# Another order of products, and a transfer in place of a sum, in the last group of a two-layer attention trunk

## The chip, the cores and the metric

The kernel runs on one core of one Trainium2 chip. The metric is the device time of one execution in microseconds (us); the time of a kernel is the median of its runs. TensorE does the matrix products, VectorE (DVE in the rows) and ScalarE (ACT) the elementwise work, GpSimd (POOL) issues some of the transfers and SyncE (SP) most of them.

## The reference

Two layers over 256 tokens of 2048 channels. Each layer normalises its input and multiplies it by one wide weight matrix; two causal token mixers work on the result, and their gated outputs are merged and added to the residual stream.

```python
h = rms_norm(x, norm_gain)
proj = jnp.einsum('bsd,de->bse', h, w_in)
(da_q, da_k, da_v, da_z, sb_q, sb_k, sb_v, sb_z,
 gate_a, gate_b) = split_columns(proj)
...
ub = stick_breaking_attention(qs, ks, vs) * jax.nn.silu(sb_z)

y = (jax.nn.sigmoid(gate_a) * jnp.einsum('bse,ed->bsd', ua, w_branch_a)
     + jax.nn.sigmoid(gate_b) * jnp.einsum('bse,ed->bsd', ub, w_branch_b))
return x + jnp.einsum('bsd,de->bse', y, w_out)
```

Everything is float32. The segments of `proj` that matter here are `sb_v` and `sb_z` (2048 columns each) and the two gates.

## The kernel before

**Precision.** A float32 product is made of three TensorE matmuls (`mm3`, lines 70 to 72): each operand is split into a high part, rounded by ScalarE (line 65, tiles `wh`), and a low part, subtracted by VectorE (line 66, tiles `wl`). A weight slice of 128 x 1024 (512 KB, two k-steps of 512 columns) is loaded by SyncE's queue (line 93) into one of 12 `raw` buffers, split, and used. There are 4 buffers `wh` and 3 `wl`.

**Two kinds of streams.** A `c_stream` multiplies the 256 tokens by one chunk of 512 columns in 8 steps of 12 matmuls (`mc` in the accumulator memory). An `s_stream` makes two chunks at once, with seven products of half depth in place of eight (Strassen's scheme in Winograd's form): 28 steps of 6 matmuls. Its weight halves are b11, b21 (first chunk) and b12, b22 (second chunk), four slices each. The left-hand sums s(0) to s(3) were made earlier (`sm`); the right-hand sums are made in place, in the raw buffers of b11 (`xs`) and b22 (`zs`), slice by slice, each after the step that has read the slice's old value. Such a sum is either an accumulating transfer, issued on GpSimd's queue (line 169, b12 or b22 is read again from memory and added), or one VectorE instruction on two buffers (line 173). The accumulators are sU, sN and sQ, one buffer each.

**The two orders.** A flag `tb_dma` chooses.

With the flag, the products follow as a(0,0) into sU; s(3) into sN, each step followed by the transfer zs += b12; s(0) into sQ, each step followed by the transfer xs += b22; s(2) into a new sQ; s(1) into sU, added to what is there; a(1,0) into sN; a(1,1) into sQ.

Without it, s(3) is followed by nothing; each step of s(0) is followed by the VectorE sum xs += zs and then by the transfer zs += b12; s(1) comes before s(2). In both cases ScalarE copies s(0)'s result out of sQ into p5 (line 218) before sQ is used again, and VectorE's lines 227, 230 and 236 take the results of s(1), s(3) and s(2) on.

**Where they run.** Each layer has four stick-breaking groups of four heads. For group g, `sb_weights(g)` makes the attention weights (scores; lines 659 to 670 on ScalarE and VectorE; transposes on TensorE at line 548), then one `s_stream` makes the group's `sb_v` and `sb_z` chunks, interleaved by `run` with a chain of two `c_stream`s of 8 steps and 2 idle steps each: the next group's queries and keys, whose results are transposed on TensorE (line 277), or, in the last group, two chunks of gate a, whose results go through a sigmoid (line 716) to memory (line 717). `run` advances the stream that is behind, 20 steps against 28. The last group also splits reloaded values `ua`. Behind the last group come three more `s_stream`s for gates, without the flag, interleaved with the branch products (the gate blocks).

The program is laid out by a planner that simulates it and orders each engine's instructions by priority; splits and sums are raised in priority. So an engine's order isn't always that of the text.

Of the kernel before, what the change touches and what calls it, by code (L numbers as in the profile page):

```python
# [23 lines left out]
NG = D // CW  # L24
# [18 lines left out]
def trunk(ctx: ExitStack, tc: tile.TileContext, x, xT, norm_gain, w_in, qk_gain, lam_vecs,  # L43
# [14 lines left out]
    def heads(ap):  # L58
        return ap.rearrange("p (h d) -> p h d", d=HD)
# [196 lines left out]
    def run(*streams):  # L256

        live = [[n, 0, g] for n, g in streams]
        while live:
            s = min(live, key=lambda s: (s[1] + 0.5) / s[0])  # L260
            if next(s[2], "end") == "end":
                live.remove(s)
            s[1] += 1

    def chain(*gens):
        for g in gens:
            yield from g
# [144 lines left out]
    for l in range(DEPTH):  # L412
# [37 lines left out]
        def w_chunk(base, g):  # L450
            return [w_in[l, base + g, kp] for kp in range(KP)]
# [133 lines left out]
        def vz_fin(v, gz, after_z=None):  # L585

            def fin_v(t, op):
                n = tok()
                op(n)
                split(v[0][:, t], v[1][:, t], n)  # L590

            def fin_z(t, op):
                op(gz[:, t])
                if t == NT - 1:
                    gf = gz.rearrange("p t d -> p (t d)")
                    nc.scalar.activation(out=gf, in_=gf, func=AF.Silu)
                    if after_z is not None:
                        after_z()
            return fin_v, fin_z
# [18 lines left out]
        def v_tiles():  # L618
            return (att.tile([P, NT, CW], F32R, name="vh"), att.tile([P, NT, CW], F32R, name="vl"))
# [32 lines left out]
        def sb_weights(g):  # L652
            wT = attn_pair()
            table(EXP_LN)
            for t in range(NT):
                for hs in ([[0, 1, 2, 3]] if t == 0 else [[0, 1], [2, 3]]):
                    sm, nk = scores(qT[NG + g], kT[NG + g], hs, t, masks["strict"])
                    e = tok()
                    nc.scalar.activation(out=e, in_=sm, func=AF.Abs)
                    nc.scalar.activation(out=e, in_=e, func=AF.Exp, scale=-1.0)  # L660
                    nc.scalar.activation(out=e, in_=e, func=AF.Ln, bias=1.0)
                    rl = tok()
                    nc.scalar.activation(out=rl, in_=sm, func=AF.Relu)
                    for i in range(len(hs)):
                        lo, hi = i * nk, (i + 1) * nk
                        rv = slice(hi - 1, lo - 1 if lo else None, -1)
                        nc.vector.tensor_tensor_scan(out=e[:, rv], data0=e[:, rv], data1=rl[:, rv],
                                                     initial=0.0, op0=ALU.add, op1=ALU.add)
                    nc.vector.tensor_tensor(out=sm, in0=sm, in1=e, op=ALU.subtract)
                    nc.scalar.activation(out=sm, in_=sm, func=AF.Exp)  # L670
                    attn_T(sm, wT, hs, t)
            return wT

        def sb_out(g, wT, v, gzT):
            keep = g == NG - 1
            if keep:
                uh, ul = u_parts()
            else:
                us = att.tile([P, HPG, S], F32, name="us", tag="aTh")
            for hp in range(0, HPG, 2):  # L680
                o = ps_at.tile([P, CW], F32, name="at")
                ov = o.rearrange("p (h q) -> p h q", q=S)
                for i in range(2):
                    h = hp + i
                    vs = slice(h * HD, (h + 1) * HD)
                    mm3(ov[:, i], v[0][:, 0, vs], v[1][:, 0, vs], wT[0][:, h, 0:2].rearrange(
                        "p b q -> p (b q)"), wT[1][:, h, 0:2].rearrange("p b q -> p (b q)"),
                        True, False)
                    mm3(ov[:, i, P:], v[0][:, 1, vs], v[1][:, 1, vs], wT[0][:, h, 2], wT[1][:, h, 2],
                        False, True)  # L690
                hs = slice(hp, hp + 2)
                uv = tok().rearrange("p (h q) -> p h q", q=S) if keep else us[:, hs]
                nc.vector.tensor_tensor(out=uv, in0=ov, in1=gzT[:, hs], op=ALU.mult)
                if keep:
                    split(uh[:, hs], ul[:, hs], uv)
            if keep:
                return uh, ul
            spill("b", g, us)
# [30 lines left out]
        def q_stream(n, xin, alt=False, gap=0):  # L729
            f, base = (da_fin, DA_Q) if n < NG else (sb_fin, SB_Q)  # L730
            return c_stream(w_chunk(base, n % NG), xin, f("q", n % NG), alt, gap)

        def k_stream(n, xin, alt=False, gap=0, before=None):
            f, base = (da_fin, DA_K) if n < NG else (sb_fin, SB_K)
            return c_stream(w_chunk(base, n % NG), xin, f("k", n % NG), alt, gap, before)
# [27 lines left out]
        def reload(b, groups, u):  # L763
            for g in groups:
                raw = load_raw(u_dram[b][:, g * 4:(g + 1) * 4].rearrange("p h s -> p (h s)"))
                ts = [att.tile([P, 4, S], F32R, name="u" + b, tag=tag) for tag in GZ_TAGS[g]]
                split(ts[0], ts[1], raw.rearrange("p (h s) -> p h s", s=S))
                for i in range(2):
                    u[i][g] = ts[i]

        def gate_chunk(b, c):
            return c_stream(w_chunk(GATE_A if b == "a" else GATE_B, c), xt, sig_fin(b, c), False,
                            GAP)

        ua, ub = ([None] * NG, [None] * NG), ([None] * NG, [None] * NG)
        for g in range(NG):
            wT = sb_weights(g)
            if g == NG - 1:
                reload("a", (0, 1), ua)
            v = v_tiles()  # L780
            gz = att.tile([P, NT, CW], F32, name="gz")
            gzT = []

            def z_T():
                gzT.append(att.tile([P, HPG, S], F32, name="gzT", tag="hold"))
                for t in range(NT):
                    tr = ps_at.tile([P, CW], F32, name="at")
                    for h in range(HPG):
                        nc.tensor.transpose(out=tr[:, h * P:(h + 1) * P],
                                            in_=gz[:, t, h * P:(h + 1) * P], identity=ident)  # L790
                    nc.scalar.copy(gzT[0][:, :, t * P:(t + 1) * P], heads(tr))

            fv, fz = vz_fin(v, gz, z_T)
            s = s_stream(w_chunk(SB_V, g), w_chunk(SB_Z, g), xt, sm,
                         lambda col, t, op: (fv, fz)[col](t, op), g + 1 < NG)
            if g + 1 < NG:
                c = [q_stream(NG + g + 1, xt, False, GAP), k_stream(NG + g + 1, xt, False, GAP)]
            else:
                c = [gate_chunk("a", 0), gate_chunk("a", 1)]
            run((len(c) * (C_STEPS + GAP), chain(*c)), (S_STEPS, s))  # L800
            last_u = sb_out(g, wT, v, gzT[0])
# [154 lines left out]
```

## Time and profile before

| | |
|---|---|
| median of 3 runs | 2382.98 us (2380.82 to 2383.87) |
| the profiled execution | 2380.12 us, span 2378.4 us |
| instructions | 31466 |
| TensorE matmul busy | 2356.9 us, 99% of the span |
| VectorE, ScalarE, GpSimd busy | 1781.6, 1529.9 and 341.1 us |
| read from memory, written | 509.35 and 24.12 MB |

The profiled execution is one of its own, not among the three runs. Its span runs from the first to the last recorded instruction. Busy shares are of the span; TensorE's matmuls overlap, so their starts tell more than their lengths.

### The profile page before, as it was taken

What the parts mean: (1) busy time and instruction counts of PE and PEld (TensorE: products, weight loads), DVE (VectorE), ACT (ScalarE), POOL (GpSimd) and SP (SyncE); (2) the same over time, 40 slices, a digit from 0 to 9 for tenths busy, and PEclk for the clock granted to TensorE, in tenths of its full rate; (3) what the DMA queues carried; (4) which work ended last, traced back from release to release, by engine and by line L of the source; (5) the groups of instructions that cost most, each with busy time, mean ns of one, the idle gap of its engine ahead of it and who ended that gap; (6) DMA issues with size and microseconds to landing.
All of it is one profiled execution on the core that took longest, in us unless ns stands there. A gap on an engine that the chain in (4) does not pass through costs nothing.

```text
span 2378.4 us, 31466 instructions
## 1 busy us (share of the span) xinstructions
PE 2356.9 (99%) x10996; PEld 1955.5 (82%) x10996; DVE 1781.6 (75%) x2000; ACT 1529.9 (64%) x2201; POOL 341.1 (14%) x399
## 2 busy tenths in 40 slices
PE   9999999999999999999999999999999999999999
PEld 7888888888888888788888888888888888887887
DVE  6777768688788888786566777676887887878854
ACT  7666666677777666554465666666767776656643
POOL 1231220201101011100020312202011010111000
PEclk9999999999999999999999999999999999999999
DMA  9546546878877888898665465468789778988972
GB/s 367 179 143 210 196 142 221 198 224 235 238 234 209 266 274 247 293 287 271 207 211 177 142 213 187 141 226 209 224 233 241 234 210 254 289 237 285 298 264 89
DMA packets 152239, 535.55 MB, mean 225 GB/s; under 512 B 17360, under 2 KB 17872, under 8 KB 152080
## 3 DMA queue, kind: packets, MB, share of 16 engines
q1 hardware_dynamic: 123552, 432.72, 53.3%
q0 software_dynamic: 28096, 100.42, 19.9%
q8 instruction: 86, 1.41, 0.2%
q14 instruction: 73, 0.60, 0.1%
q10 hardware_dynamic: 432, 0.40, 0.1%
HBM read 509.35 MB, written 24.12 MB: 224 GB/s over the span
## 4 chain that ended last, share of the span: by engine, by line
PE 96%; DMA 2%; DVE 1%; ACT 1%; issue 0%; DVEq 0%; SPq 0%; ACTq 0%
PE mc L71 16%; PE mc L72 16%; PE mc L70 16%; PE sU L71 6%; PE sU L72 5%; PE sU L70 5%; PE sN L71 5%; PE sN L72 5%; PE sN L70 5%; PE sQ L71 3%; PE sQ L70 3%; PE sQ L72 3%; PE at L277 2%; PE at L71 1%; PE at L72 1%; PE at L70 1%
## 5 line engine op out<-in xcount | busy, mean ns | idle before, releaser
L66 DVE TENSOR_TENSOR wl<-raw,wh 128x1024 fp32r<-128x1024 f32 (+1 forms) x1001 | 1212.5, 1222 | 391.9 <-PE mc L71 155.9
L65 ACT CAST wh<-raw 128x1024 fp32r<-128x1024 f32 (+1 forms) x1001 | 1047.5, 1051 | 642.2 <-PE mc L72 340.7
L169 POOL DMA_DIRECT2D raw<-in_w_in x136 | 117.8, 867 | 835.4 <-DVE wl L66 429.3
L71 PE MATMUL mc<-wl,xTh 128*128 128x512 f32 x576 | 225.1, 391 | 2.5 <-DVE wl L66 2.4
L72 PE MATMUL mc<-wh,xTl 128*128 128x512 f32 x576 | 224.4, 390 | 0.0
L70 PE MATMUL mc<-wh,xTh 128*128 128x512 f32 x576 | 206.8, 391 | 0.0
L70 PE MATMUL mc<-wh,xrh 128*128 128x512 f32 x512 | 197.6, 393 | 5.7 <-ACT wh L65 5.7
L71 PE MATMUL mc<-wl,xrh 128*128 128x512 f32 x512 | 200.5, 392 | 0.0
L72 PE MATMUL mc<-wh,xrl 128*128 128x512 f32 x512 | 200.3, 392 | 0.0
L71 PEld LDWEIGHTS mc<-wl,xTh 128*128 128x128 f32 x576 | 108.1, 188 | 26.2 <-DVE wl L66 4.2
L70 PEld LDWEIGHTS mc<-wh,xTh 128*128 128x128 f32 x576 | 107.7, 188 | 22.7 <-ACT wh L65 0.6
L72 PEld LDWEIGHTS mc<-wh,xTl 128*128 128x128 f32 x576 | 108.2, 188 | 21.9
L70 PEld LDWEIGHTS mc<-wh,xrh 128*128 128x128 f32 x512 | 96.6, 189 | 25.5 <-ACT wh L65 5.7
L173 DVE TENSOR_TENSOR raw<-raw 128x1024 f32<-128x1024 f32 x88 | 107.2, 1221 | 13.3 <-DMA raw<-in_w_in 12.2
L71 PEld LDWEIGHTS mc<-wl,xrh 128*128 128x128 f32 x512 | 96.6, 189 | 19.5 <-DVE wl L66 0.2
L72 PEld LDWEIGHTS mc<-wh,xrl 128*128 128x128 f32 x512 | 96.5, 188 | 19.3
L71 PE MATMUL sU<-wl,xrh 128*128 128x512 f32 x256 | 100.7, 393 | 0.1
L72 PE MATMUL sN<-wh,xrl 128*128 128x512 f32 x256 | 100.3, 392 | 0.0
L70 PE MATMUL sN<-wh,xrh 128*128 128x512 f32 x256 | 100.1, 391 | 0.0
L71 PE MATMUL mc<-wl,ua 128*128 128x512 f32 x256 | 100.0, 390 | 0.0
L71 PE MATMUL sN<-wl,xrh 128*128 128x512 f32 x256 | 100.0, 390 | 0.0
L70 PE MATMUL sU<-wh,xrh 128*128 128x512 f32 x256 | 100.0, 390 | 0.0
(254 smaller groups left out, 4913.6 us busy)
## 6 DMA issues: line engine op xcount, KB each, us to landing
raw<-in_w_in SPq DMA_DIRECT2D x583, 512.0 KB, 4.4
raw<-in_w_in POOLq DMA_DIRECT2D x136, 512.0 KB, 7.6
raw<-in_w_a SPq DMA_DIRECT2D x64, 512.0 KB, 5.3
raw<-in_w_b SPq DMA_DIRECT2D x64, 512.0 KB, 5.8
raw<-in_w_o SPq DMA_DIRECT2D x64, 512.0 KB, 4.5
ua<-us POOLq DMA_DIRECT2D x8, 512.0 KB, 5.9
raw<-ua SPq DMA_DIRECT2D x8, 512.0 KB, 4.8
siga<-tok POOLq DMA_DIRECT2D x16, 256.0 KB, 5.3
```

The lines of the kernel that those rows point to most:

```text
L65: nc.scalar.copy(h, src)
L66: nc.vector.tensor_tensor(out=l, in0=src, in1=h.bitcast(F32), op=ALU.subtract)
L70: nc.tensor.matmul(ps, lhsT=lh, rhs=rh, start=start, stop=False, **kw)
L71: nc.tensor.matmul(ps, lhsT=lh, rhs=rl, start=False, stop=False, **kw)
L72: nc.tensor.matmul(ps, lhsT=ll, rhs=rh, start=False, stop=stop, **kw)
L169: nc.gpsimd.dma_start(out=dst, in_=src, accum_op=ALU.add)
L173: nc.vector.tensor_tensor(out=dst, in0=dst, in1=src, op=ALU.add)
L277: nc.tensor.transpose(out=tr[:, j * P:(j + 1) * P], in_=src[:, j * P:(j + 1) * P], identity=ident)
```

## The change

In the four groups of a layer, the flag `tb_dma` was true for the first three and false for the last; now it is true for all four. The gate blocks keep the other order.

```diff
             fv, fz = vz_fin(v, gz, z_T)
             s = s_stream(w_chunk(SB_V, g), w_chunk(SB_Z, g), xt, sm,
-                         lambda col, t, op: (fv, fz)[col](t, op), g + 1 < NG)
+                         lambda col, t, op: (fv, fz)[col](t, op), True)
             if g + 1 < NG:
                 c = [q_stream(NG + g + 1, xt, False, GAP), k_stream(NG + g + 1, xt, False, GAP)]
             else:
                 c = [gate_chunk("a", 0), gate_chunk("a", 1)]
```

## Rows read from the trace of the kernel before

**Rows 1.** The page, part 1: busy time, share, instructions.

```profile
PE 2356.9 (99%) x10996; PEld 1955.5 (82%) x10996; DVE 1781.6 (75%) x2000; ACT 1529.9 (64%) x2201; POOL 341.1 (14%) x399
```

**Rows 2.** The page, part 4: the chain that ended last.

```profile
PE 96%; DMA 2%; DVE 1%; ACT 1%; issue 0%; DVEq 0%; SPq 0%; ACTq 0%
```

**Rows 3.** Windows: length, busy PE, PEld, DVE, ACT, POOL; clock; DMA share; GB/s.

```profile
1750.00:1880.00 130.00, 130.00 (x620) 108.30 (x619) 106.83 (x111) 93.79 (x112) 12.63 (x15) 1.00 0.83 232
700.00:815.00 115.00, 113.57 (x548) 94.54 (x547) 94.70 (x98) 83.64 (x98) 12.35 (x16) 1.00 0.81 235
1885.00:2000.00 115.00, 113.57 (x548) 94.58 (x547) 94.93 (x99) 83.89 (x98) 12.42 (x16) 1.00 0.83 235
815.00:1080.00 265.00, 261.44 (x1155) 214.62 (x1154) 217.57 (x204) 159.83 (x168) 30.33 (x43) 1.00 0.89 275
2000.00:2270.00 270.00, 268.66 (x1187) 220.03 (x1186) 222.26 (x210) 161.91 (x171) 29.30 (x41) 1.00 0.88 273
```

**Rows 4.** Timeline of TensorE, layer 1's last group: start, us, what.

```profile
1941.30 0.39 PE L72 MATMUL sQ<-wh,sml 128*128 128x512 f32 x1
1942.34 0.50 PE L71 MATMUL sU<-wl,smh 128*128 128x512 f32 x1 [0.66 <-DVE wl L66]
1942.67 0.39 PE L72 MATMUL sU<-wh,sml 128*128 128x512 f32 x1
...
1943.83 0.62 PE L70 MATMUL mc<-wh,xTh 128*128 128x512 f32 x2
1944.61 0.50 PE L71 MATMUL sU<-wl,smh 128*128 128x512 f32 x1 [0.16 <-DVE wl L66]
...
1945.87 0.40 PE L70 MATMUL sU<-wh,smh 128*128 128x512 f32 x1
1946.89 0.66 PE L548 MATMUL at<-ident,tok 128*128 128x128 f32 x4 [0.62 <-ACT tok L670]
```

**Rows 5.** Timeline of VectorE, the stretch of rows 4.

```profile
1938.77 1.22 DVE L173 TENSOR_TENSOR raw<-raw 128x1024 f32<-128x1024 f32 x1
...
1942.20 1.22 DVE L173 TENSOR_TENSOR raw<-raw 128x1024 f32<-128x1024 f32 x1
...
1944.47 0.68 DVE L669 TENSOR_TENSOR tok<-tok 128x512 f32<-128x512 f32 x1
```

**Rows 6.** Timeline of ScalarE, the stretch of rows 4.

```profile
1941.27 1.99 ACT L65 CAST wh<-raw 128x1024 fp32r<-128x1024 f32 x2
1943.16 0.59 ACT L218 COPY pp<-sQ 128x512 f32<-128x512 f32 x1
...
1944.91 1.28 ACT L670 ACT_TABLE_LOAD   x1
```

**Rows 7.** The page: line 173's group (part 5); accumulating transfers' landing (part 6).

```profile
L173 DVE TENSOR_TENSOR raw<-raw 128x1024 f32<-128x1024 f32 x88 | 107.2, 1221 | 13.3 <-DMA raw<-in_w_in 12.2
...
raw<-in_w_in POOLq DMA_DIRECT2D x136, 512.0 KB, 7.6
```

**Rows 8.** Windows: second product of layer 1's third and last group.

```profile
1820.00:1836.00 16.00, 16.00 (x77) 13.39 (x76) 13.31 (x14) 12.14 (x17) 4.33 (x6) 1.00 1.00 219
1911.00:1927.00 16.00, 16.00 (x77) 13.36 (x77) 13.31 (x15) 12.15 (x17) 0.70 (x1) 1.00 0.47 129
```

**Rows 9.** Waits of TensorE, whole span: total us, times, longest.

```profile
PE at L548 <- ACT tok L670: 1.2, 2, 0.6
...
PE sQ L70 <- ACT pp L218: 1.0, 2, 0.5
```

**Rows 10.** Timelines of TensorE and ScalarE, layer 1's second group.

```profile
1758.57 1.04 PE L277 MATMUL at<-ident,tok 128*128 128x128 f32 x8
...
1760.10 0.41 PE L70 MATMUL sQ<-wh,smh 128*128 128x512 f32 x1
...
1759.38 0.58 ACT L218 COPY pp<-sQ 128x512 f32<-128x512 f32 x1
```

**Rows 11.** Timeline of TensorE, layer 1's first group.

```profile
1692.95 0.50 PE L71 MATMUL mc<-wl,xTh 128*128 128x512 f32 x1 [0.69 <-DVE wl L66]
```

## The prediction

> **What bounds it now.** I read the page of the profile first. TensorE is busy for 2356.9 of 2378.4 us [rows 1], and the chain of waits runs through TensorE for 96% of the span [rows 2]. So there are 21.5 us of visible idle time in all, part of it before the first weights land and after the last matmul; no saving on another engine can be worth more than the TensorE waits that it ends. The changed stretch is the last stick-breaking group, once per layer. In the windows view it keeps TensorE busy for 113.57 of 115 us, to the same hundredth in both layers, while the second and third group of layer 1 together show 130.00 of 130 [rows 3]. So the last group idles 1.43 us a layer that its neighbours, which already have the order of the change, don't.
>
> The timeline shows what the 1.43 us are [rows 4]. Back-to-back 512-column matmuls start 0.23 us apart (two take 0.62 us, one 0.39). From 1941.30 to 1942.34 is 1.04 us, so 0.81 are lost; the next start comes 0.33 later, so another 0.10 go in refilling the pipeline. From the two matmuls at 1943.83, which end their turn at 1944.29, to 1944.61 is 0.32, with a second 0.10 taken for the refill. From 1945.87 to 1946.89 is 1.02, so 0.79 are lost. Together 2.12 us a layer, 4.2 us in two. The first two losses wait for VectorE's low halves (wl): VectorE spent 1938.77 to 1939.99 and 1942.20 to 1943.42 in the sums of line 173 [rows 5]. The third waits for ScalarE's exp of line 670, which itself waited for the subtraction of line 669; VectorE reached that only at 1944.47 [rows 5], and after it ScalarE loaded a table for 1.28 us [rows 6].
>
> **The change, part by part.** Removed: four VectorE sums xs += zs a layer, eight in all of the 88 of line 173, at 1.22 us each [rows 7]: 4.9 us of VectorE a layer, 9.8 in all. VectorE isn't the bound, so these count only through the waits above. The sums sit between the instructions that the three stalls wait for; without them line 669 comes at least the 1.22 us of the sum at 1942.20 sooner, and 2.4 with the one at 1938.77, against a stall of 0.79. I take all three stalls as ended: 2.12 us a layer. The lower bound is that the third stays, as the table load stays: 1.33.
>
> Added: four accumulating transfers a layer, 512 KB each, 4 MB over the run. Each z sum is now issued behind its step of the second product rather than of the third, and each third sum takes the place that the z sum had. On GpSimd's queue both stand in order with the stores of the gate's sigmoid, so a late sigmoid holds back the third sums behind it. What covers this: a z sum is read eight steps later (rest of the second product, third, then fourth), a third sum eight steps later as well (rest of the third, the fourth, then the fifth). A step is six matmuls of its own plus its share of the other stream, 12 matmuls for each of 16 working steps against 28 steps: (6 + 12 x 16/28) x 0.23 = 3.0 us, so eight steps give 24 us, against 7.6 us from issue to landing [rows 7]. The transfer engines have room: in the second product their share is 0.47 here and 1.00 in the third group, where TensorE is nevertheless busy 16.00 of 16 us [rows 8]. Cost taken: nothing. If the cover failed, TensorE would wait for the excess of the landing over 24 us.
>
> Moved: the product with s(2) now follows s(0) directly, in the same accumulator sQ. Its first matmul has to wait until ScalarE has copied p5 out of sQ, and ScalarE has casts queued in front of that copy, so what is late next is the whole TensorE queue behind that matmul. Before, the four steps of s(1) into sU lay between them. This is the new wait. The trace shows it in the first group: 1.0 us in two waits, the longest 0.5 [rows 9]. In the second group it is nearly covered: the copy runs from 1759.38 and the product starts at 1760.10, with eight transposes of the query chunk filling 1.04 us from 1758.57 [rows 10]. The last group's other stream makes gate chunks, which end in a sigmoid and a store and give no such transposes; and the first chunk's end with its two idle steps falls on this very boundary (step 12 of 28 against step 8 of 20). So I take the second group's picture without its transposes, 1.04 us, plus 0.10 of refill: 1.1 us a layer. The lower bound is nothing, as in the third group. The upper one is the last group's own clock: the matmul at 1941.30 gives way at 1941.53, and the copy that began at 1943.16 ends at 1943.75 [rows 6], so 2.2 us, 2.3 with refill, if nothing fills it.
>
> A rule of the Trainium skill speaks against this order: PSUM — Partial Sum Buffer, in its summary of rules for kernel authors, says to let matmuls run into another bank than the one being read. The waits on line 218 agree with it. By the rule alone, with nothing to fill the gap, the change would come out as the second rival below, at no gain.
>
> Both corrections of column z and w now fall together, after s(1): three VectorE instructions in a row, between which a wl split stands. In the first group that burst stalls TensorE for 0.69 us [rows 11], in the next two not at all [rows 3]. I take nothing, and keep 0.7 and 0.1 of refill as the bound.
>
> Sum: 2.12 saved less 1.1 is 1.0 us a layer, 2.0 in all. The profiled execution took 2380.12 us, 1.7 more than its span; it becomes 2378.1. It lies 2.9 under the median of 2382.98, so the median becomes 2381.0.
>
> **The rivals.** First, the whole gain: the wait for p5 is covered, as in the third group. Then 4.2 us go, and the median becomes 2378.7. For it speaks that two of three groups with this order lose nothing visible; against it, the missing transposes. To pass the 0.2% it needs the gate blocks behind to change too: they idle 3.56 us in layer 0 and 1.34 in layer 1 [rows 3], by transfers that land late at times. If layer 0 became like layer 1, 2.2 more would go, to 2376.5.
>
> Second, no gain: the wait for p5 is unfilled at 2.3 us a layer and takes the place of 2.12. The median becomes 2383.4. If the third stall also stayed, 2385.
>
> Third, slower: ScalarE's order at the boundary. The planner that lays out each engine's order may put more in front of the copy of p5: the table load of 1.28 us and another cast of 1.0 (two took 1.99) [rows 6]. The wait is then 2.3 + 2.3 = 4.6 us a layer, and the median rises by 2 x (4.6 - 2.1) = 5.0 to 2388. The sign turns from a wait of 2.1 us on, and it can be measured from 4.5 us on. For it speaks that ScalarE works its queue in order and has these very instructions within 3 us of the copy; against it, that in three groups the copy stood behind one or two casts alone.
>
> Fourth, the transfers: if the four more in the second product delay the loads of the gate blocks, layer 1's stretch may become like layer 0's, 2.2 us more: 2383.2 with the forecast's sum.
>
> **How the numbers follow.** About 0.2%, 4.8 us, is what a measurement of this kernel can tell from no change. Forecast 0.45, whole gain 0.22, no gain 0.18, slower 0.08, transfers 0.07. Faster by over 0.2% takes half of the whole gain's chance (that with calmer gate blocks): 0.11. Slower takes the third rival and a little of the others: 0.10. Within 0.2%: 0.79. The range runs from the whole gain with calmer gate blocks, 2376.5, to between the no-gain case and the third rival, 2387.5. The forecast's own range, by the bounds of its terms, is 2378.7 to 2385.
>
> **What would show it.** Line 173 has 80 sums and line 169 has 144 transfers. Right: in the last groups TensorE no longer waits for wl or line 670, and a wait of about 1 us on line 218 stands in their place at the start of the second sQ product, once a layer. The windows of the last group then show 114 to 114.5 of 115 us busy. Wrong: that wait is over 2 us or absent, the waits for wl stay although the sums are gone, matmuls of s(1) or s(2) wait for an accumulating transfer, or the idle time of the gate blocks moves by more than the last group's.

## The result and the profile after

The changed kernel takes 2391.26 us (2390.13 to 2395.34), the kernel before 2382.65 beside it (now the median of five runs). The recorded ratio is 1.0045, 95% interval 1.0033 to 1.0056; the two medians alone give 1.0036, which is 8.6 us. So the change makes the kernel slower, where the forecast was 2381.0 and the range ended at 2387.5. The profiled execution of after has a span of 2390.0 us, 11.6 more than that of before.

The counts are those foretold, 80 sums and 144 transfers; the page's group of line 173, and the landing of the accumulating transfers [rows 7]:

```profile
L173 DVE TENSOR_TENSOR raw<-raw 128x1024 f32<-128x1024 f32 x80 | 97.5, 1221 | 9.0 <-DMA raw<-in_w_in 7.9
...
raw<-in_w_in POOLq DMA_DIRECT2D x144, 512.0 KB, 7.8
```

The windows of after, columns as in [rows 3]: the last group of layer 0 and of layer 1, layer 0's gate blocks, then the second product of layer 1's last group [rows 8], and the ten microseconds in which the third product ends:

```profile
700.00:815.00 115.00, 109.97 (x511) 91.09 (x510) 88.41 (x91) 81.70 (x96) 14.86 (x19) 0.97 0.87 240
1895.00:2010.00 115.00, 109.42 (x512) 90.52 (x511) 88.43 (x91) 81.82 (x96) 15.74 (x20) 0.97 0.87 238
815.00:1080.00 265.00, 261.40 (x1160) 214.20 (x1159) 216.50 (x203) 159.17 (x167) 31.21 (x44) 1.00 0.88 274
1918.00:1934.00 16.00, 16.00 (x77) 13.40 (x76) 13.30 (x15) 12.15 (x17) 4.33 (x6) 1.00 1.02 230
1949.00:1959.00 10.00, 5.03 (x15) 3.68 (x14) 5.23 (x7) 7.17 (x10) 1.18 (x3) 0.66 1.03 270
```

The last group loses TensorE 5.0 and 5.6 of 115 us where it lost 1.43 [rows 3], and the granted clock in it is 0.97. The gate blocks behind it are as before (261.40 against 261.44). The loss has one place, which the timeline of TensorE shows, the counterpart of [rows 4]:

```profile
1945.58 0.39 PE L70 MATMUL sQ<-wh,smh 128*128 128x512 f32 x1
1946.58 0.50 PE L71 MATMUL sQ<-wl,smh 128*128 128x512 f32 x1 [0.61 <-DVE wl L66]
1946.91 0.40 PE L72 MATMUL sQ<-wh,sml 128*128 128x512 f32 x1
...
1949.01 0.39 PE L72 MATMUL sQ<-wh,sml 128*128 128x512 f32 x1
1954.36 1.12 PE L548 MATMUL at<-ident,tok 128*128 128x128 f32 x4 [4.97 <-ACT tok L670]
1955.30 1.22 PE L70 MATMUL mc<-wh,xTh 128*128 128x512 f32 x2
1956.32 0.63 PE L70 MATMUL sQ<-wh,smh 128*128 128x512 f32 x1
1956.74 0.63 PE L71 MATMUL sQ<-wl,smh 128*128 128x512 f32 x1
...
1958.45 0.50 PE L72 MATMUL sQ<-wh,sml 128*128 128x512 f32 x1
1958.78 0.40 PE L70 MATMUL sQ<-wh,smh 128*128 128x512 f32 x1
```

The matmul at 1949.01 is the last of s(0). What follows it in TensorE's order all hangs on ScalarE: the transposes of line 548 on the exp of line 670, two matmuls of the next gate chunk on a cast, and the product with s(2) on the copy of p5. From 1949.01 to 1954.36 is 5.35 us, so 5.12 are lost. Then the matmuls start 0.43 us apart, not 0.23: the lower of the two clock levels, 1.2 GHz. Layer 0 shows the same, the same 4.97 us of wait, and ten such slow sQ matmuls where layer 1 has six. Of the old stalls the two on sU are gone; a new one on wl stands at 1946.58 (0.77, and 0.10 of refill). The wait that the prediction named is absent: for the copy of line 218 the waits view of after has the very line of [rows 9], 1.0 us in two waits, and both are in the layers' first groups.

ScalarE's timeline over that stretch [rows 6] says why the exp is late:

```profile
1939.73 1.05 ACT L65 CAST wh<-raw 128x1024 fp32r<-128x1024 f32 x1 [5.03 <-DMA raw<-in_w_in]
...
1941.16 2.00 ACT L65 CAST ua<-raw 128x1024 fp32r<-128x1024 f32 x2
1943.06 0.63 ACT L659 ACTIVATE tok<-tok 128x512 f32<-128x512 f32 x1
...
1948.11 1.28 ACT L716 ACT_TABLE_LOAD   x1
...
1952.39 1.28 ACT L670 ACT_TABLE_LOAD   x1
1953.68 0.63 ACT L670 ACTIVATE tok<-tok 128x512 f32<-128x512 f32 x1
...
1955.15 0.58 ACT L218 COPY pp<-sQ 128x512 f32<-128x512 f32 x1
```

From 1939.73 on ScalarE has no idle time until it has copied p5. It starts that burst late, because the cast at its head waits 5.03 us for a weight load; and the burst holds the two casts of `ua`, the chain of the attention weights, two sigmoids, five more weight casts and two table loads ahead of the exp. VectorE's line 669 is not the cause: it was done at 1950.78, before the second table load began.

```profile
1950.09 0.69 DVE L669 TENSOR_TENSOR tok<-tok 128x512 f32<-128x512 f32 x1
```

The load for the cast was issued at 1932.29; its row of the transfers (queue, size, us to landing):

```profile
raw<-in_w_in SPq DMA_DIRECT2D x1, 512.0 KB, 7.3
```

### The profile page after: what moved, and what is told of

Read it like the earlier page. It is cut to its first block, busy times and chain, and to the rows that moved or that the text cites. A ratio compares the mean times of both kernels' runs of the same rounds, so it can differ in the third digit from the quotient of the medians.

```text
span 2390.0 us, 31482 instructions
## 1 busy us (share of the span) xinstructions
PE 2361.6 (99%) x10996; PEld 1959.2 (82%) x10996; DVE 1774.6 (74%) x1992; ACT 1529.6 (64%) x2201; POOL 347.8 (15%) x407
## 4 chain that ended last, share of the span: by engine, by line
PE 95%; DMA 2%; DVE 1%; ACT 1%; issue 1%; POOL 0%; DVEq 0%; ACTq 0%; POOLq 0%
PE mc L71 16%; PE mc L70 16%; PE mc L72 16%; PE sU L70 6%; PE sU L71 6%; PE sU L72 5%; PE sN L71 5%; PE sN L72 5%; PE sN L70 5%; PE sQ L71 3%; PE sQ L70 3%; PE sQ L72 3%; PE at L277 2%; PE at L71 1%; PE at L72 1%; PE at L70 1%
## 5 line engine op out<-in xcount | busy, mean ns | idle before, releaser
L169 POOL DMA_DIRECT2D raw<-in_w_in x144 | 124.5, 866 | 838.7 <-DVE wl L66 565.2
L173 DVE TENSOR_TENSOR raw<-raw 128x1024 f32<-128x1024 f32 x80 | 97.5, 1221 | 9.0 <-DMA raw<-in_w_in 7.9
```

What stands on the lines that cost most here:

```text
L169: nc.gpsimd.dma_start(out=dst, in_=src, accum_op=ALU.add)
L173: nc.vector.tensor_tensor(out=dst, in0=dst, in1=src, op=ALU.add)
```

## The experiments

Ten are edits of the changed kernel, two of the kernel before. The table gives their times, the ratio to the kernel before on the same chip (its median there 2380.3 to 2380.9), TensorE's busy time in the windows 700 to 815 and 1895 to 2010 us, and the clock in them. Busy time and clock are those of the one profiled execution of each, which can lie off the median: 3.6 us below it in run 1, 3.7 above it in run 2.

| | median us | ratio [95%] | busy of 115 us, layers 0, 1 | clock |
|---|---|---|---|---|
| kernel before | | | 113.57, 113.57 | 1.00, 1.00 |
| changed | 2391.26 | 1.0045 [1.0033, 1.0056] | 109.97, 109.42 | 0.97, 0.97 |
| 1 no z sums | 2385.70 | 1.0021 [1.0012, 1.0030] | 111.87, 111.87 | 0.99, 1.00 |
| 2 order alone | 2389.08 | 1.0038 [1.0025, 1.0050] | 109.33, 110.92 | 0.99, 0.99 |
| 3 sums alone | 2393.58 | 1.0052 [1.0039, 1.0065] | 110.05, 110.81 | 0.99, 0.97 |
| 4 no table switch | 2386.34 | 1.0024 [1.0014, 1.0034] | 112.57, 110.83 | 0.99, 1.00 |
| 5 late reload | 2388.06 | 1.0026 [1.0016, 1.0037] | 111.16, 111.16 | 0.99, 0.97 |
| 6 late reload, no idle steps | 2380.83 | 0.9997 [0.9988, 1.0006] | 113.92, 113.96 | 1.00, 1.00 |
| 7 order alone, stores by ScalarE | 2389.53 | 1.0035 [1.0021, 1.0049] | 110.66, 110.79 | 1.00, 0.99 |
| 8 before with late reload | 2377.33 | 0.9984 [0.9975, 0.9992] | 114.89, 114.87 | 1.00, 1.00 |
| 9 cuts 1 and 4 | 2378.13 | 0.9990 [0.9981, 0.9999] | 114.33, 114.33 | 1.00, 1.00 |
| 10 no idle steps | 2382.34 | 1.0008 [0.9999, 1.0016] | 112.72, 113.47 | 1.00, 1.00 |
| 11 before with late reload, no idle steps | 2378.66 | 0.9994 [0.9985, 1.0002] | 113.94, 113.70 | 1.00, 1.00 |
| 12 cut 4, late reload | 2377.82 | 0.9989 [0.9980, 0.9998] | 114.21, 114.21 | 1.00, 1.00 |

By their intervals runs 2, 3 and 7 can't be told from the changed kernel, and the gain of run 5 is hardly clear of the noise.

**1. The z sums left out.**

```diff
         yield from prod(n_ps, s(3), loader(zs, b22),
-                        (lambda i: add_dma(zs[i], b12[i])) if tb_dma else None)
+                        (lambda i: add_dma(zs[i], b12[i])) if tb_dma and "z" not in skip else None)
```

(`skip` is "z" in the last group alone.)

> The changed kernel with the four accumulating transfers zs += b12 of the last group's second product left out in each layer (column z of that group then lacks them); the orders of TensorE and ScalarE stay those of the changed kernel. Theory 1 (the transfers crowd the loads): the weight load of 7.35 us lands in about 4, the cast behind it no longer waits 5.0 us at the head of ScalarE's queue, the exp of line 670 comes in time, and the waits of TensorE on it fall from 5.0 to under 1.5 us a layer with full clock behind them: 2379 to 2383 us. Theory 2 (the order of ScalarE's instructions alone, with two table loads ahead of the exp): wait and time stay, 2390 to 2392 us.

The load now lands in 3.3 us (first row below, the same load as the 7.3 above), and no cast of the last group waits for one. But TensorE still waits 2.85 us at the boundary in each layer: neither theory, about half of each. The timeline of TensorE in both layers:

```profile
raw<-in_w_in SPq DMA_DIRECT2D x1, 512.0 KB, 3.3
```

```profile
759.15 0.66 PE L548 MATMUL at<-ident,tok 128*128 128x128 f32 x4 [2.85 <-ACT tok L670]
760.09 1.22 PE L70 MATMUL mc<-wh,xTh 128*128 128x512 f32 x2 [0.28 <-ACT wh L65]
761.11 0.63 PE L70 MATMUL sQ<-wh,smh 128*128 128x512 f32 x1
761.53 0.63 PE L71 MATMUL sQ<-wl,smh 128*128 128x512 f32 x1
...
1945.51 0.66 PE L548 MATMUL at<-ident,tok 128*128 128x128 f32 x4 [2.85 <-ACT tok L670]
1946.45 0.73 PE L70 MATMUL mc<-wh,xTh 128*128 128x512 f32 x2 [0.28 <-ACT wh L65]
1947.02 0.42 PE L70 MATMUL sQ<-wh,smh 128*128 128x512 f32 x1
1947.27 0.39 PE L71 MATMUL sQ<-wl,smh 128*128 128x512 f32 x1
```

The same wait is followed by slow matmuls (0.42 apart) in layer 0 and by full speed (0.25 and less) in layer 1. So layer 1 prices the slow clock of the changed kernel: from line 548's start to the seventh sQ matmul is 4.42 us there (1954.36 to 1958.78), here 2.92 (1945.51 to 1948.43). Of these 0.59 are the short wait on wh: 0.94 us from line 548's start to the next matmul, 0.35 in run 6 below, where nothing is waited for. The slow clock costs 4.42 - 2.33 = 2.1 us in layer 1. This profiled execution was the fastest of the eleven; whether in the others the slow clock followed in both layers is not shown.

**2 and 3. One part at a time.** A second flag separates the order from the sums:

```diff
-    def s_stream(sl, sr, xh, sm, fin, tb_dma=False):
+    def s_stream(sl, sr, xh, sm, fin, tb_dma=False, v_first=None):
...
-        hk = KP // 2
+        hk, v_first = KP // 2, tb_dma if v_first is None else v_first
...
-        if tb_dma:
+        if v_first:
             v_ps = ps_s.tile([P, CW], F32, name="sQ")
```

Run 2 calls it with `g + 1 < NG, True`, run 3 with `True, g + 1 < NG`; the other two tests of the flag behind it change alike.

> The new order of products in the last group, but the sums as before: after each step of s(0) VectorE adds zs to xs and a transfer adds b12 to zs. Theory 1: no transfers in the second product, so loads land in time; the old waits for wl stay in part and the wait for p5 of about 1 us a layer comes in: 2382 to 2386 us, and no wait over 2 us at line 548. Theory 2: the order of products is what hurts: 2388 to 2392 us.

> The new sums (both by transfers) in the old order of products, s(1) before s(2). Theory 1: the loads are as late as in the changed kernel, the cast still holds ScalarE's queue for 4 to 5 us, and TensorE's transposes of line 548 wait 2 to 5 us a layer: 2386 to 2391 us. Theory 2: the boundary is gone with the order, and the three old waits with the sums: 2378 to 2381 us.

Neither part is harmless alone, but the two runs don't price the parts. Each half of the change leaves one kind of sum a cover of four steps where the whole change gives eight: in run 2 the z sums, in run 3 the third sums. So each brings a wait of its own, and the two don't add up. In run 2 the boundary is nearly clean, but each z sum is now issued after VectorE's sum in the product before the one that reads it. Layer 1's timelines (TensorE, GpSimd, ScalarE):

```profile
1949.69 0.50 PE L70 MATMUL sQ<-wh,smh 128*128 128x512 f32 x1 [0.68 <-ACT pp L218]
...
1954.77 0.50 PE L70 MATMUL sQ<-wh,smh 128*128 128x512 f32 x1 [1.17 <-ACT wh L65]
```

```profile
1947.81 0.58 POOL L717 DMA_DIRECT2D siga<-tok  x1 [6.87 <-ACT tok L716]
...
1948.38 0.90 POOL L169 DMA_DIRECT2D raw<-in_w_in  x1
```

```profile
1953.67 1.99 ACT L65 CAST wh<-raw 128x1024 fp32r<-128x1024 f32 x2 [4.03 <-DMA raw<-in_w_in]
```

The third z sum, issued at 1948.38, took 5.2 us, and the cast that reads it stood 4.03 us at ScalarE's head, with the exp behind it. The copy of p5 alone, the prediction's one term for the new order, is the 0.68 in the first row. In run 3 the load is late as in the changed kernel (a cast waits 4.61 us). But with s(1) directly behind s(0), TensorE's longest wait in layer 1 comes from something else: a cast for s(1) waits 2.90 us more, for the third of the sums xs += b22. That sum was issued at 1948.26 and took 7.4 us. The exp of line 670 stands behind this cast and a table load (GpSimd, ScalarE, TensorE):

```profile
1948.26 0.87 POOL L169 DMA_DIRECT2D raw<-in_w_in  x1 [7.64 <-DVE wl L66]
```

```profile
1955.79 1.04 ACT L65 CAST wh<-raw 128x1024 fp32r<-128x1024 f32 x1 [2.90 <-DMA raw<-in_w_in]
```

```profile
1956.88 0.79 PE L70 MATMUL sU<-wh,smh 128*128 128x512 f32 x1 [1.75 <-ACT wh L65]
1958.82 1.12 PE L548 MATMUL at<-ident,tok 128*128 128x128 f32 x4 [1.15 <-ACT tok L670]
```

Slow matmuls follow. The time is above both theories' ranges. The late load of the first theory is there, but the late sum was in neither.

**4. No table switch.** This run leaves the sigmoid out: with Relu in its place no table load stands between the gate chunk's end and the exp of line 670 in the trace.

```diff
-                    nc.scalar.activation(out=g, in_=ps[t], func=AF.Sigmoid)
+                    nc.scalar.activation(out=g, in_=ps[t], func=AF.Relu)
```

> The changed kernel with Relu in place of the sigmoid in the two gate chunks beside the last group (their gate values are then wrong), so that two table loads of 1.28 us each fall away ahead of the exp of line 670; all else keeps its order. Theory 1: the exp comes 2.6 us sooner, the wait at line 548 falls from 5.0 to about 2.4 us a layer, and the cast still waits 5.0 us for its load: 2386 us if the half clock behind the wait stays, 2380 if it goes with the shorter wait. Theory 2: the table loads are the cause: wait under 1 us, 2379 to 2381 us.

The first theory held: the cast still waits 4.0 us for its load, and the wait at line 548 falls from 4.97 to 2.15, by 2.8, for two table loads of 1.28. The time is the upper of its two figures: the slow clock still followed in layer 0; in layer 1 it didn't, but there TensorE lost another 1.3 us to a wait for wl. ScalarE: Activation LUTs of the Trainium skill (Table sets: the hidden batching unit) tells authors to batch activations by table set; the saving agrees. The rows put a switch at 1.28 us here, not at the about 2.7 that this section gives for one.

**9. Both cuts**, with TensorE's and ScalarE's instructions in the order of run 4:

> Both cuts at once: the z sums of the last group left out and Relu in place of the sigmoid in its gate chunks (column z and the gate values are then wrong); TensorE's and ScalarE's orders are those of the run with Relu alone. Theory now: at the boundary of the two sQ products TensorE has nothing else to do until ScalarE has worked off its burst, and two things make that late, the late load and the two table loads; each cut alone left 2.3 to 3.0 us a layer, both together leave 0 to 1 at line 548 and about 0.5 at the mc product behind it, with full clock: 2377 to 2381 us. Rival (the order holds TensorE up whatever precedes it): the wait at line 548 stays above 2 us, 2384 us or more.

It held. The waits view of the four kernels, in one line each (total, times, longest): changed, run 1, run 4, run 9.

```profile
PE at L548 <- ACT tok L670: 9.9, 2, 5.0
```

```profile
PE at L548 <- ACT tok L670: 5.7, 2, 2.8
```

```profile
PE at L548 <- ACT tok L670: 4.3, 2, 2.2
```

```profile
PE at L548 <- ACT tok L670: 0.8, 2, 0.4
```

The transfers carry 2.1 us a layer of the wait, the table loads 2.8, and together they take away 4.6 of 5.0. With the wait the slow clock is gone too.

**5 and 8. The reload moved** behind the group, in the changed kernel and in that before:

```diff
-                reload("a", (0, 1), ua)
...
-        reload("a", (2, 3), ua)
+        reload("a", (0, 1, 2, 3), ua)
```

> The changed kernel with the reload of ua (two raw buffers and two casts on ScalarE, 2.0 us) moved behind the last group, beside the other reload. Theory now: the last group's transfers hurt because the reload holds two of the 12 raw buffers, so that each load is used one load earlier than in the third group. Then the cast waits no load, ScalarE's burst is 2 us shorter, and the wait of the transposes at line 548 falls from 5.0 us to 0 to 1.5 a layer, without half clock: 2379 to 2383 us. Rival (the transfers alone make the loads late): the cast still waits over 4 us for its load, and the wait at line 548 stays above 2.5 us: 2386 to 2390 us.

> The kernel before with the reload of ua moved behind the last group, as the control for the other two. Theory: the reload costs nothing there, since the old order keeps the transfer engines at 0.47 in the second product; the stalls of 2.1 us a layer stay or shrink by the 2 us of ScalarE's casts: 2379 to 2382 us. Rival (the reload is a burden in either version): 2376 to 2378 us.

Run 5's time is its rival's, its mechanism neither's. The loads still take 6.2 to 8.2 us, but no weight cast of the last group waits for one: with the reload holding no raw buffers, a load is issued further ahead of its use. So it takes both, the transfers and the reload, to make a cast wait. Yet TensorE stops at the same place, one instruction later (TensorE, then ScalarE):

```profile
1944.22 0.60 PE L548 MATMUL at<-ident,tok 128*128 128x128 f32 x4
1948.66 1.22 PE L70 MATMUL mc<-wh,xTh 128*128 128x512 f32 x2 [3.84 <-ACT wh L65]
```

```profile
1940.05 1.28 ACT L716 ACT_TABLE_LOAD   x1
...
1941.96 1.28 ACT L670 ACT_TABLE_LOAD   x1
...
1944.84 1.28 ACT L716 ACT_TABLE_LOAD   x1
...
1946.63 1.98 ACT L65 CAST wh<-raw 128x1024 fp32r<-128x1024 f32 x2
```

The planner moved the exp between the two sigmoids, which makes three table loads, and the next weight cast stands behind the third. In the kernel before, the same move helps (run 8, its rival): the stalls of [rows 4] go and TensorE is busy for 114.9 of 115 us. Run 8 beats both kernels, by 0.16% of the one before.

**12. The late reload without table switches.**

> The changed kernel with the late reload and with Relu in place of the sigmoid in the last group's gate chunks (their gate values are then wrong). With the late reload alone TensorE still stood 4.1 us a layer at the boundary behind three table loads of 1.28 us, with no late load at all. Theory: without those 3.8 us the wait falls to under 0.6 us a layer and the clock stays full: 2378 to 2381 us. Rival (the weight casts that follow the second sigmoid are late for another reason, a buffer or a load): over 2 us stay, 2383 us or more.

The wait at the boundary falls from 3.84 to 0.79 us, the clock stays full. The wait is a little over the 0.6 expected, the time a little under its range.

**6, 10, 11. The gate chunks without idle steps**, so that the first one ends two steps behind the boundary: with the late reload, without it, and in the kernel before with it.

```diff
             return c_stream(w_chunk(GATE_A if b == "a" else GATE_B, c), xt, sig_fin(b, c), False,
-                            GAP)
+                            0)
...
-            run((len(c) * (C_STEPS + GAP), chain(*c)), (S_STEPS, s))
+            run((len(c) * (C_STEPS + GAP * (g + 1 < NG)), chain(*c)), (S_STEPS, s))
```

> As the run with the late reload, and the last group's gate chunks without their two idle steps each, so that the first chunk's end, with its sigmoid and its table load, falls two steps behind the boundary of the two sQ products. Here the exp of line 670 and the copy of p5 stand ahead of the sigmoid in ScalarE's order, and one of the table loads falls away. Theory: nothing is left at the boundary but the copy itself, under 1 us a layer; all stalls of the last group together 1 to 2 us a layer in place of 8.9: 2377 to 2380 us. Rival (the loads are late anyway): a wait on wh of 2 us or more appears somewhere in the third product: 2384 us or more.

> The changed kernel with the two idle steps behind each of the last group's gate chunks taken out, the reload left where it is: the end of the first gate chunk falls two steps behind the boundary. ScalarE copies p5 ahead of the sigmoid here, but the exp of line 670 stays between the two sigmoids, with three table loads. Theory: it is the meeting of the gate chunk's end with the boundary that costs; the stall at the boundary falls from 8 us to 1 to 3 us a layer: 2381 to 2385 us. Rival (the late load behind the reload is the larger half): waits of 3 us or more on wh or on line 670 stay, 2386 to 2390 us.

> The kernel before with both: late reload and no idle steps behind the gate chunks. If the idle steps matter only where the new order puts its boundary, this equals the kernel before with the late reload, 2376 to 2379 us, with 1 to 2.3 us of stalls in the last group; if the shorter chunks help by themselves, 2374 to 2376 us; if they bring the sigmoids against another product, 2380 us or more.

In run 6 all the change's transfers are there and the engines are as full, but the boundary costs nothing (windows; TensorE's timeline); the time is 0.8 us above the expected range:

```profile
1911.00:1927.00 16.00, 16.00 (x77) 13.39 (x76) 13.03 (x15) 12.51 (x17) 4.49 (x6) 1.00 1.04 233
```

```profile
1941.55 0.60 PE L548 MATMUL at<-ident,tok 128*128 128x128 f32 x4
1941.90 0.48 PE L70 MATMUL sQ<-wh,smh 128*128 128x512 f32 x1
```

Run 10 came out as the theory had it and shows the idle steps as the larger half: without them alone the changed kernel is no longer measurably slower. Not all of that is the meeting point: in the new layout the cast also waits less for its load, 1.6 us in layer 1 in place of 5.0. Runs 6 and 11 differ by the change alone: 0.9997 and 0.9994 to the kernel before, so with the collision gone the change is worth nothing that can be measured. Run 11 gains nothing on run 8.

**7. The order alone, the stores on ScalarE's queue.**

```diff
-                    nc.gpsimd.dma_start(out=sig_d[b, c][:, t], in_=g)
+                    nc.scalar.dma_start(out=sig_d[b, c][:, t], in_=g)
```

> The new order with the old sums, as in the run with the order alone, but the stores of the gate's sigmoid issued by ScalarE in place of GpSimd. Theory: in that run the z sums stood behind these stores in GpSimd's queue and landed 3 to 4 us too late for the product with s(2); now they are issued behind their own sums, the waits on wh in the product with s(2) shrink from 1.4 and 1.7 us to under 0.5, and the time falls from 2389 to 2383 to 2386 us. Rival (four steps are too short a cover whatever the queue): the waits stay and so does the time, 2388 to 2391 us.

The rival held. The third z sum was issued at 1945.99, 2.4 us sooner, but took 6.8 us, and the cast waited longer:

```profile
1952.91 2.00 ACT L65 CAST wh<-raw 128x1024 fp32r<-128x1024 f32 x2 [5.07 <-DMA raw<-in_w_in]
```

So four steps are too short a cover here, with the stores ahead of the sums in GpSimd's queue and without them, and run 3 shows the same for the third sums. The new order and the new sums belong together.

## Why the prediction was wrong

Two steps failed: the added transfers, put at nothing, and the price of the new boundary. A third term was missing.

**Removed: 2.12 us a layer saved.** Partly right. Both waits for wl on sU went; a new one on sQ came (0.87 in layer 1, 0.32 in layer 0), which run 1, without the late load, doesn't have. The third stall, on line 670, was tied to VectorE's line 669; ScalarE's own queue decided when the exp came, and it grew from 0.79 to 5.12. The rows before the change already say so: line 669 was done at 1945.15 [rows 5], while the table load ran until 1946.19 [rows 6], and the exp came right behind the load:

```profile
1946.20 0.63 ACT L670 ACTIVATE tok<-tok 128x512 f32<-128x512 f32 x1
```

**Added: nothing.** This is the first step that failed. The cover of eight steps was right: no matmul waited for an accumulating transfer. But the term asked only when the transfers land, not what they do to the plain loads beside them: 7.3 us in place of 3.3. The third group was taken as proof that a full set of transfer engines is harmless. In the trace of after that group has as late a load (7.0 us), but no reload that holds two raw buffers, so there the cast comes later. Price: 2.1 us of wait a layer, by run 1.

**Moved: 1.1 us a layer.** This is the second, and the larger. It looked for one wait, that of p5's copy. As a price for that wait alone 1.1 is fair: where it shows it is 0.68 us (run 2) and 0.97 (run 7). In the changed kernel it doesn't show at all, as TensorE stops earlier. What matters is what else TensorE has at the point where the two sQ products meet: the transposes and the next chunk's first matmuls, which wait for the same ScalarE. In the order before, four steps of s(1) stood there as cover. The prediction saw that the gate chunk's end falls on this boundary and counted in this term only that it brings no transposes, not that it brings two sigmoids and two table loads in front of the exp. Price: the other 3 us of the wait.

**Not in the sum: the slow clock.** 2.1 us in layer 1 by run 1. In layer 0 it is 6.13 us from line 548's start at 761.39 to the eleventh sQ matmul at 767.52; in run 1's layer 1 it is 3.83 less 0.59 (1945.51 to 1949.34), so 2.9.

**The sum by these terms.** Layer 1: 5.12 + 2.1 + 0.87 - 2.12 = 6.0; layer 0: 5.14 (756.02 to 761.39, less 0.23) + 2.9 + 0.32 - 2.12 = 6.2. Together 12.2 us, against 11.6 between the spans. The medians differ by 8.6, as the profiled execution of before was 2.5 us faster than its median and that of after 0.5 slower. The forecast's own upper bound of 2385 leaves out the 0.8 us a layer that it kept for VectorE's burst; with it that bound is 2386.5, still below the result.

**The rivals.** The third came nearest: ScalarE's order at the boundary, a table load and a cast ahead, 4.6 us a layer and 2388. Engine and place were right; the waiting instruction was line 548 and not the copy, and the clock was missing. That its price is so near the measured 5.12 is partly luck: 2.1 of the 5.12 come from the late load, which this rival doesn't have. The fourth looked for late loads in the gate blocks, which did not change; the late load was in the group itself.

## What to carry to other kernels

Ask of a new boundary not only what its one dependence costs, but what everything behind it in the engine's order waits for; if it is all one other engine's queue, price that whole queue, table loads included. A stage that ran well with full transfer engines proves it only for its own lead of loads: count the free buffers before carrying it over. And where two events meet by a step count, try moving the meeting point first: here that took the measurable loss away, with the transfers left as they were. When the two halves of a change are run one by one, look whether each half keeps the cover that the whole has; here neither did.

## What the runs showed of the hardware

Accumulating transfers slowed the plain loads beside them from 3.3 to 7.3 us for 512 KB, with the transfer engines' share in the second product going from 0.47 (run 1) to 1.02 (changed kernel). DMA: Bandwidth & Descriptors of the Trainium skill (Queues, rings and completion order) says that each transfer engine takes turns between the queues that have work; the row agrees with that, and no run shows the turns themselves.

A wait of 2.85 us in both layers of one execution (run 1), with the same instructions around it, was followed by matmuls at half speed once and at full speed once; so was one of 2.15 us in run 4. After 5 us (changed kernel) half speed followed in both layers, after 0.8 us (run 12) full speed in both. After 3.84 us (run 5) one layer was slow at once; in the other, four matmuls ran at full speed before eight slow ones. What decides between them stays open.
